# Low weight parts from a negated copy and an adding transfer, in place of a subtraction

## The chip, the core and the metric

The kernel runs on one core of a Trainium2 chip. TensorE (PE, with its weight loads as PEld), VectorE (DVE), ScalarE (ACT), GpSimd (POOL) and the queue that issues plain transfers (SP) run side by side and wait for each other by semaphores; sixteen DMA engines move data between memory and the on-chip buffers. The metric is the device time of one execution in microseconds. Three runs of the kernel before took 1635.21, 1635.33 and 1636.85 us; the median is 1635.33.

## The reference, cut to what matters

One inference step of an encoder layer with 1024 channels, for 512 prompt frames and 64 sample frames together (T = 576 columns):

```
h = LN1(alpha*x + 0.5*FFN1(x))
z = h @ w_in      # mLSTM q,k,v,o,i,f | attention q,k,v | branch gates g_m, g_a
h = LN2(alpha*h + (sig(g_m)*(mLSTM(z) @ w_ml_proj) + sig(g_a)*(Attn(z) @ w_att_proj)) @ w_out)
y = LN3(alpha*h + 0.5*FFN2(h))
```

All arrays are float32. PE multiplies in a reduced type (fp32r), so each operand is split into two: hi, the operand rounded to that type, and lo = operand - hi. A product is then three: hi*hi + hi*lo + lo*hi. This document is about how lo of the weights is made.

## The kernel before

Activations lie with channels on the 128 partitions, in eight slices of 128 channels (k = 0 to 7) and two halves of columns (256 and 320). Weights come in tiles of 128 x 1024 float32, 512 KB: for one block of 128 output channels, the eight slices side by side. `plan` lists all tiles in the order of use, as (key, source in memory): FFN1; the in-projection `("in", c)`, 72 tiles, with the narrow gate tile `"if"` among them; the attention projection `("ap", j)`, the mLSTM projection `("mp", j)` and the output projection `("o", j)`, 8 tiles each; FFN2.

`pump` (line 170) works down this list. It issues SP's load of a tile into a raw buffer (`wr`, two of them; line 178) and, later, converts it: ACT writes hi (`wh`, four buffers; `act`, line 137) and DVE writes lo = raw - hi (`wl`, four buffers; `tt`, line 140). Seven tiles, those in `PIECES`, are converted in two pieces of 512 columns; two of them, in `ON_POOL`, have lo made by POOL. The raw buffer is free for the next load when both hi and lo have been written. A pair of `wh` and `wl` is free when PE has done its last product with it (`done`). So a tile's conversion can begin when the tile four places before it has been used up.

`gemm` takes tiles and runs the products: for each slice k and each half, hi*hi, hi*lo, lo*hi into one PSUM bank, 48 matmuls for a tile. Normally it goes tile by tile. Where LN1 has finished only its first half, the first in-projection tiles go as a group, `WAVE_M`: v, k and q of the first pair of heads (`("in", 48)`, `("in", 40)`, `("in", 32)`) in turn within each slice on the first half, then the gate tile on the first half, then the same on the second half. All four tiles are held to the end of the group. They hold all four `wh` buffers, and the conversion of the next tile, `("in", 49)`, waits for the first of them.

After the group come, in this order: attention (eight head pairs, tiles v, k, q each, with scores, softmax and value products put between the in-projection's matmuls), the attention branch's gates (64 to 71), the attention projection, the mLSTM by four heads (8 tiles each), the mLSTM branch's gates (56 to 63), the mLSTM projection, the output projection with LN2, FFN2.

PE's order is written out by hand: a planner (`Order`) keeps a model of PE's time, and work that depends on other engines (transposes, scores, statistics) is put in with `later(delay, ...)`. The order on the other engines is made by a list scheduler from priorities (`hot` raises them; `pump` runs at 30, normalisation steps at 300) and a model of times. Each engine then executes its list strictly in order. ACT also copies products out of PSUM and computes all exponentials and sigmoids; POOL makes k copies (`kh`, `kl` in `dup`), two of the eight subtractions of the mean and the power -0.5 in the layer norms, and small copies and fills; in this kernel POOL issues no transfer.

Of the kernel before, what the change touches and what calls it, by code (L numbers as in the profile page):

```python
# [14 lines left out]
ALU = mybir.AluOpType  # L15
# [66 lines left out]
def tile_layer(ctx: ExitStack, tc: tile.TileContext, ins, outs):  # L82
    nc = tc.nc
    PE, ACT, DVE, POOL, SP = nc.tensor, nc.scalar, nc.vector, nc.gpsimd, nc.sync
# [12 lines left out]
    def hot(off):  # L97
        def wrap(fn):
            def run(*a, **k):
                with tc.high_priority(offset=off):  # L100
                    return fn(*a, **k)
            return run
        return wrap

    def nm(s):
        uid[0] += 1
        return f"{s}_{uid[0]}"
# [7 lines left out]
    def f(ap):  # L115
        return ap.bitcast(F32)

    def hs(t, hf):
        t0, n = HALVES[hf]
        return t[:, t0:t0 + n]  # L120
# [15 lines left out]
    def act(out, in_, func=AF.Copy, **kw):  # L136
        ACT.activation(out, in_, func, **kw)  # L137

    def tt(out, a, b, op, eng=None):
        return (eng or DVE).tensor_tensor(out, a, b, op=op)  # L140
# [18 lines left out]
    NX = 10  # L159
    PIECES = {("gu2", 0, 0), ("gu2", 0, 1), ("gu2", 1, 0), ("gu2", 1, 1), ("in", 48), ("in", 40), ("in", 32)}  # L160
    ON_POOL = {("gu2", 0, 0), ("gu2", 1, 0)}
    CP = (6, 7)
    CPF = (4, 5, 6, 7)
    GR = 450
    L_MEAN, L_STATS, L_SPREAD = 300, 1440, 4920
    plan = []
# [3 lines left out]
    @hot(30)  # L170
    def pump(limit=2):
        while True:
            c = wst["conv"]
            if wst["dma"] < min(len(plan), c + 2):
                i = wst["dma"]
                raws[i] = wpool.tile([P, 1024], F32, tag="wr", name=nm("wr"), bufs=2)
                src = plan[i][1]
                SP.dma_start(raws[i][:, :src.shape[1]], src)
                wst["dma"] += 1
                continue  # L180
            if c < wst["stop"] and c < wst["taken"] + limit and c < wst["done"] + NWB:
                raw = raws.pop(c)
                n = plan[c][1].shape[1]
                hi = wpool.tile([P, 1024], F32R, tag="wh", name=nm("wh"), bufs=NWB)
                if plan[c][0] == "if":

                    r3 = raw[:, :n].rearrange("p (k c) -> p k c", c=64)
                    h3 = hi.rearrange("p (k c) -> p k c", c=P)
                    act(h3[:, :, 0:64], r3)
                    tt(h3[:, :, 64:128], r3, f(h3[:, :, 0:64]), ALU.subtract)  # L190
                    parts[c] = (hi, None)
                else:
                    lo = wpool.tile([P, 1024], F32R, tag="wl", name=nm("wl"), bufs=NWB)
                    step = n if plan[c][0] not in PIECES else 512
                    for a in range(0, n, step):
                        act(hi[:, a:a + step], raw[:, a:a + step])
                        tt(lo[:, a:a + step], raw[:, a:a + step], f(hi[:, a:a + step]), ALU.subtract,
                           POOL if plan[c][0] in ON_POOL else DVE)
                    parts[c] = (hi, lo)
                wst["conv"] += 1  # L200
                continue
            return

    def take(key):
        c = wst["taken"]
        assert plan[c][0] == key, (plan[c][0], key)
        wst["taken"] += 1
        if wst["conv"] <= c:
            pump(1)
        assert c in parts  # L210
        later(300, pump)
        return c

    def done(c):
        del parts[c]
        wst["done"] += 1
        later(50, pump)
# [149 lines left out]
    for k0 in range(0, KT, 2):  # L367
        ww = slice(k0 * P, (k0 + 2) * P)
        for c in (0, 1, 2):
            hi, lo = parts[c]  # L370
# [14 lines left out]
    class Norm:  # L385
# [97 lines left out]
        def centre(self, hf, bc, power):  # L483
            mb = hs(self.c0, hf)
            act(mb, bc)
            with tc.issue_after(power.ins):
                for j in range(KT):
                    dh = hs(self.d[j], hf)
                    tt(dh, dh, mb, ALU.subtract, POOL if j in (CPF if self.final is not None and hf else CP) else DVE)

# [632 lines left out]
    mp = mstack.enter_context(tc.tile_pool(name="ml", bufs=1, reuse_waits="tile"))  # L1123
# [403 lines left out]
```

## Time and profile before

The profiled execution took 1635.94 us; its span, from the first to the last instruction, is 1634.2 us.

| what | value |
|---|---|
| median of three runs | 1635.33 us |
| profiled execution, its span | 1635.94 us, 1634.2 us |
| mean granted PE clock | 0.988 |
| busy: PE, DVE, ACT, POOL | 98%, 67%, 50%, 9% of the span |
| DMA engines | 27.3% of 16 engines' span, mean 90 GB/s |
| read from memory, written | 135.37 MB, 9.24 MB |
| PE idle, longest single releaser | ACT s, 9.3 us in 3 waits |

Names in the rows are tiles of the program: `wr` raw weights, `wh` and `wl` hi and lo of the weights, `mm` and `aux` PSUM banks. A row "wl<-wr,wh" writes lo from raw and hi. A value such as "[3.97 <-PE mm L123]" is the idle time of the engine just before the instruction, and what ended it. Times in rows of order are us from the span's start.

### The profile page before, as it was taken

What the parts mean: (1) busy time and instruction counts of PE and PEld (TensorE: products, weight loads), DVE (VectorE), ACT (ScalarE), POOL (GpSimd) and SP (SyncE); (2) the same over time, 40 slices, a digit from 0 to 9 for tenths busy, and PEclk for the clock granted to TensorE, in tenths of its full rate; (3) what the DMA queues carried; (4) which work ended last, traced back from release to release, by engine and by line L of the source; (5) the groups of instructions that cost most, each with busy time, mean ns of one, the idle gap of its engine ahead of it and who ended that gap; (6) DMA issues with size and microseconds to landing.
All of it is one profiled execution on the core that took longest, in us unless ns stands there. A gap on an engine that the chain in (4) does not pass through costs nothing.

```text
span 1634.2 us, 29320 instructions
## 1 busy us (share of the span) xinstructions
PE 1593.3 (98%) x11831; PEld 1567.2 (96%) x11831; DVE 1090.1 (67%) x2158; ACT 811.2 (50%) x1529; POOL 141.1 (9%) x277
## 2 busy tenths in 40 slices
PE   8999998999999999999999999999999999999997
PEld 8999998999999999999999999999999999998996
DVE  7777777535788777673656748434778777768336
ACT  6445546223566566651657466443345554545223
POOL 0000000000313323000111101002020000000001
PEclk9999999999999999999999999999989999999999
DMA  6222221224342333122222122222212222212333
GB/s 215 73 83 104 93 89 48 82 84 119 120 135 89 100 106 101 48 85 85 78 72 78 59 94 67 68 78 78 83 62 103 104 83 100 104 62 59 87 93 116
DMA packets 52320, 146.51 MB, mean 90 GB/s; under 512 B 5720, under 2 KB 16600, under 8 KB 52184
## 3 DMA queue, kind: packets, MB, share of 16 engines
q1 hardware_dynamic: 52184, 144.63, 27.3%
q8 instruction: 93, 1.52, 0.4%
q14 instruction: 43, 0.35, 0.1%
HBM read 135.37 MB, written 9.24 MB: 88 GB/s over the span
## 4 chain that ended last, share of the span: by engine, by line
PE 56%; DVE 3%; issue 1%; ACT 1%; POOL 1%; ACTq 0%; POOLq 0%; DVEq 0%
PE mm L123 51%; PE aux L123 4%; PE aux L133 1%; DVE s L140 1%; DVE h L140 0%; ACT s L137 0%; DVE wl L140 0%; DVE hc L140 0%; POOL wl L140 0%; POOL kh L147 0%; DVE s L143 0%; DVE ptl L140 0%; ACT sc L137 0%; ACT L137 0%; POOL rs L382 0%
## 5 line engine op out<-in xcount | busy, mean ns | idle before, releaser
L123 PE MATMUL mm<-s,wh 128*128 128x256 f32 (+2 forms) x3872 | 796.0, 299 | 11.4 <-ACT s L137 9.3
L123 PEld LDWEIGHTS mm<-s,wh 128*128 128x128 f32 x3872 | 624.9, 190 | 16.4 <-ACT s L137 10.1
L123 PE MATMUL mm<-s,wl 128*128 128x256 f32 (+2 forms) x1920 | 569.1, 296 | 0.0
L123 PEld LDWEIGHTS mm<-s,wl 128*128 128x128 f32 x1920 | 365.0, 190 | 0.0
L140 DVE TENSOR_TENSOR wl<-wr,wh 128x1024 fp32r<-128x1024 f32 (+2 forms) x166 | 195.9, 1183 | 186.4 <-ACT wh L137 185.8
L137 ACT ACTIVATE wh<-wr 128x1024 fp32r<-128x1024 f32 (+2 forms) x171 | 169.7, 996 | 301.5 <-PE mm L123 281.6
L123 PE MATMUL mm<-hc,wh 128*128 128x256 f32 (+1 forms) x704 | 147.7, 301 | 9.8 <-DVE hc L140 5.8
L123 PE MATMUL mm<-h,wh 128*128 128x256 f32 (+1 forms) x704 | 140.7, 294 | 0.0
L123 PEld LDWEIGHTS mm<-hc,wh 128*128 128x128 f32 x704 | 116.4, 192 | 13.2 <-DVE hc L140 8.9
L123 PE MATMUL mm<-tx,wh 128*128 128x288 f32 x624 | 128.3, 296 | 0.0
L140 DVE TENSOR_TENSOR wl<-ws,wh 128x1024 fp32r<-128x1024 f32 x39 | 47.8, 1226 | 111.1 <-ACT wh L137 111.1
L123 PEld LDWEIGHTS mm<-h,wh 128*128 128x128 f32 x704 | 112.7, 187 | 0.2
L123 PE MATMUL mm<-hc,wl 128*128 128x256 f32 (+1 forms) x352 | 105.1, 299 | 0.0
L123 PE MATMUL mm<-h,wl 128*128 128x256 f32 (+1 forms) x352 | 103.3, 294 | 0.0
L123 PEld LDWEIGHTS mm<-tx,wh 128*128 128x128 f32 x624 | 100.9, 190 | 0.0
L123 PE MATMUL mm<-tx,wl 128*128 128x288 f32 x312 | 92.8, 297 | 0.0
L137 ACT ACTIVATE wh<-ws 128x1024 fp32r<-128x1024 f32 x39 | 41.3, 1058 | 102.4 <-PE mm L123 101.7
L382 POOL TENSOR_TENSOR rs<-var,mhalf 128x2 f32<-128x2 f32 (+1 forms) x6 | 5.2, 865 | 825.0 <-DVE var L143 425.0
L123 PEld LDWEIGHTS mm<-hc,wl 128*128 128x128 f32 x352 | 67.7, 192 | 0.0
L123 PEld LDWEIGHTS mm<-h,wl 128*128 128x128 f32 x352 | 65.9, 187 | 0.0
L137 ACT ACT_TABLE_LOAD x45 | 57.7, 1283 | 5.5 <-DVE U L143 4.0
L123 PEld LDWEIGHTS mm<-tx,wl 128*128 128x128 f32 x312 | 59.1, 190 | 0.0
(282 smaller groups left out, 2864.3 us busy)
## 6 DMA issues: line engine op xcount, KB each, us to landing
wu<-in_w_gu SPq DMA_DIRECT2D x78, 512.0 KB, 4.3
wr<-in_w_in SPq DMA_DIRECT2D x72, 512.0 KB, 3.5
wr<-in_w_dn SPq DMA_DIRECT2D x40, 512.0 KB, 3.5
wr<-in_w_dn SPq DMA_DIRECT2D x20, 384.0 KB, 3.2
G<-in_rbias SPq DMA_DIRECT2D x16, 256.0 KB, 2.9
wr<-in_w_ap SPq DMA_DIRECT2D x8, 512.0 KB, 3.5
wr<-in_w_mp SPq DMA_DIRECT2D x8, 512.0 KB, 3.5
wr<-in_w_o SPq DMA_DIRECT2D x8, 512.0 KB, 3.5
```

The costliest lines, as they stand in the source:

```text
L123: PE.matmul(out, lhsT, rhs, start=start, stop=stop, **kw)
L133: PE.transpose(out, in_, idn)
L137: ACT.activation(out, in_, func, **kw)
L140: return (eng or DVE).tensor_tensor(out, a, b, op=op)
L382: return y, POOL.tensor_tensor(y, v, mhalf[:, :n], op=ALU.pow)
```

## The change

For the tiles of the in-projection (all 72), both branch projections and the output projection (24), `pump` no longer subtracts. ACT writes hi as before, then a second ACT copy writes -hi into the lo buffer, and POOL issues a transfer that reads the tile from memory a second time and adds it to what lies there: lo = -hi + w. These tiles are converted whole, the three that were in `PIECES` too. The gate tile `"if"` and the tiles of both FFNs are made as before. The raw buffer of a changed tile is read by ACT alone.

```diff
+    ADDED = ("in", "ap", "mp", "o")
...
-                    step = n if plan[c][0] not in PIECES else 512
+                    step = n if plan[c][0] not in PIECES or plan[c][0][0] in ADDED else 512
                     for a in range(0, n, step):
                         act(hi[:, a:a + step], raw[:, a:a + step])
+                        if plan[c][0][0] in ADDED:
+                            act(lo, f(hi), scale=-1.0)
+                            POOL.dma_start(lo, plan[c][1], accum_op=ALU.add)
+                            continue
                         tt(lo[:, a:a + step], raw[:, a:a + step], f(hi[:, a:a + step]), ALU.subtract,
                            POOL if plan[c][0] in ON_POOL else DVE)
```

## The prediction

> **What bounds the kernel now.** I read the page's engine totals first, then busy time by stage and the chain of waits, then the order of instructions where the changed tiles have least room.
>
> ```profile
> span 1634.2 us, 29320 instructions
> PE 1593.3 (98%) x11831; PEld 1567.2 (96%) x11831; DVE 1090.1 (67%) x2158; ACT 811.2 (50%) x1529; POOL 141.1 (9%) x277
> ...
> 418.50:445.30 26.80, 26.34 (x196) 25.82 (x195) 20.84 (x39) 12.61 (x29) 13.36 (x25) 1.00 0.31 94
> 445.30:688.00 242.70, 237.95 (x1826) 229.32 (x1825) 187.93 (x577) 157.32 (x385) 59.90 (x110) 1.00 0.32 100
> 688.00:774.00 86.00, 86.00 (x648) 85.95 (x647) 47.99 (x70) 34.35 (x48) 0.69 (x7) 1.00 0.26 83
> 774.00:1060.00 286.00, 286.00 (x2134) 278.57 (x2134) 182.76 (x392) 172.24 (x334) 32.26 (x89) 1.00 0.23 74
> 1060.00:1160.00 100.00, 98.90 (x743) 98.21 (x742) 44.11 (x68) 35.24 (x58) 13.18 (x17) 1.00 0.25 80
> 1160.00:1226.00 66.00, 63.65 (x447) 62.32 (x446) 54.16 (x119) 26.65 (x57) 10.95 (x10) 0.92 0.21 66
> ...
> PE 56%; DVE 3%; issue 1%; ACT 1%; POOL 1%; ACTq 0%; POOLq 0%; DVEq 0%
> ```
>
> A window row gives the stretch, then busy time of PE, PEld, DVE, ACT, POOL, the granted clock, the DMA share and GB/s. PE is the bound: 98% of the span, and in the chain that ended last (the last line) DVE has 3% of the span, the others less. The six stages that use the 96 changed tiles (first wave, attention, gates and attention projection, mLSTM, second gates and mLSTM projection, output and LN2) leave it idle for 0.46 + 4.75 + 0 + 0 + 1.10 + 2.35 = 8.7 us in all. That is the most that a lighter DVE could return. So the question is whether the new way of making lo makes PE wait.
>
> **The change part by part.** Per tile one DVE subtraction goes, and one ACT copy, one transfer issued by POOL and 512 KB more from memory come.
>
> ```profile
> L137 ACT ACTIVATE wh<-wr 128x1024 fp32r<-128x1024 f32 x136 | 143.9, 1060 | 215.7 <-PE mm L123 200.8 <-issue 10.7 <-DMA wr<-in_w_dn 3.3
> L140 DVE TENSOR_TENSOR wl<-wr,wh x166: 676/1224/1579, 20.8 to 1612.4; 128x1024 fp32r<-128x1024 f32 x136, 128x768 fp32r<-128x768 f32 x20, 128x512 fp32r<-128x512 f32 x10
> wr<-in_w_in SPq DMA_DIRECT2D x72, 512.0 KB, 3.5
> wr<-in_w_if SPq DMA_DIRECT2D x1, 256.0 KB, 2.7
> L178 SPq DMA_DIRECT2D wr<-in_w_in x72: 327/328/587, 406.7 to 1065.2; - x72
> ```
>
> DVE loses 96 x 1.22 = 117 us; ACT gains 96 x 1.06 = 102 us (50% to about 56%); 50 MB of loads are added. DVE is off the path, so its 117 us are worth at most the 8.7 us above.
>
> The price of the adding transfer no row shows. Below: a plain load of the same bytes lands 3.5 us after issue and its issue takes 0.33. Above: reading the weights, reading lo and writing lo one after the other, 3 x 3.5 = 10.5 us, with a POOL issue as long as its longest tile operation, 1.6 us:
>
> ```profile
> L140 POOL TENSOR_TENSOR wl<-wr,wh x4: 1296/1507/1607, 1186.4 to 1204.5; 128x512 fp32r<-128x512 f32 x4
> ```
>
> I take 5.1 us to land (3.5 plus one more pass of 512 KB at the rate of the two load rows, 2 x (3.5 - 2.7) = 1.6) and 1.0 us on POOL, inside the bounds: 6.1 us together, 3.8 to 12.1. Lo is then ready 1.06 + 6.1 = 7.2 us after hi, where DVE needed 1.22: 6 us later.
>
> **Where that is hidden.** In the pure matmul stages a tile is 48 matmuls and lasts 86.0 x 48 / 648 = 6.4 us. With four buffers, hi of a tile starts when the fourth tile before it is released, so three tiles, 19.1 us, lie between that and its use; 1.06 + 7.2 = 8.3 us fit. Attention and mLSTM put other matmuls between the tiles and have more room. The cover gone, each us beyond 19.1 would cost the 40 tight tiles (gates, second gates, three projections, 8 each) one us each.
>
> **Where it is not hidden: two places, both at the first wave.** This matmul group takes v, k, q of the first head pair and the gate tile together, in the slices of k in turn.
>
> ```profile
> 410.57 0.63 ACT L137 ACTIVATE wh<-wr 128x512 fp32r<-128x512 f32 x1 [1.53 <-DMA wr<-in_w_in]
> 417.64 1.15 ACT L137 ACTIVATE wh<-wr 128x512 fp32r<-128x512 f32 x2 [1.39 <-DMA wr<-in_w_in]
> 418.38 1.29 DVE L140 TENSOR_TENSOR wl<-wr,wh 128x512 fp32r<-128x512 f32 x2
> 418.15 0.58 POOL L799 MEMSET rows<- 128x576 f32 x1 [3.28 <-PE mm L123]
> 418.75 0.28 PE L123 MATMUL mm<-s,wl 128*128 128x256 f32 x1
> 419.11 0.28 PE L123 MATMUL mm<-s,wl 128*128 128x256 f32 x1
> 419.47 0.28 PE L123 MATMUL mm<-s,wl 128*128 128x256 f32 x1
> ```
>
> The third tile's lo is written from 418.38 and PE wants it at 419.47. After the change its raw load starts earlier, when hi of the first tile (410.57 + 1.06) frees the buffer instead of DVE's last piece, and lands near 415.4. ACT then has 3 hi and 3 lo (6.4 us) from 410.57, between LN1's activations (some 3.4 us in the same stretch):
>
> ```profile
> L137 ACT ACTIVATE s<-s,cols 128x256 fp32r<-128x256 f32 x8 | 3.7, 500 | 2.3 <-DVE s L143 2.3
> ...
> 418.70 0.49 ACT L137 ACTIVATE s<-s,cols 128x256 fp32r<-128x256 f32 x1
> ```
>
> So -hi of the third tile ends between 417.5 (weights first) and 420.4 (LN first); I take 419.0. Plus 6.1 is 425.1: PE waits 5.6 us (1.9 to 13). The transfer issue may also stand behind POOL's memsets, which end near 419.5; that is in the range. LN1's activations slip by up to 3.2 us if the weights go first; the last of them, at 418.70, is wanted for the eighth slice, 7 x 1.08 us after 418.5, so that costs nothing. Everything later is queued on PE behind this wait, LN1's second statistics too, so it is all paid.
>
> ```profile
> 441.93 2.01 ACT L137 ACTIVATE wh<-wr 128x1024 fp32r<-128x1024 f32 x2 [3.97 <-PE mm L123]
> 443.02 2.36 DVE L140 TENSOR_TENSOR wl<-wr,wh 128x1024 fp32r<-128x1024 f32 x2 [3.39 <-ACT wh L137]
> 444.81 2.42 POOL L147 TENSOR_SCALAR kh<-kf 64x576 fp32r<-64x576 f32 x2 [8.51 <-ACT kf L137]
> 445.34 0.28 PE L123 MATMUL mm<-s,wl 128*128 128x256 f32 x1
> ```
>
> The wave holds all four buffers to its end, so hi of the next tile waits for PE until 441.93, and PE wants its lo at 445.34. Now lo was ready at 444.24, 1.1 us ahead. Then: -hi ends 443.0 + 1.06 = 444.1, plus 6.1 is 450.2: PE waits 4.8 us (2.6 to 10.8). The tile after it is converted 2.1 us later on ACT and has the whole next product as cover.
>
> **The clock.** PE's gaps cost twice here:
>
> ```profile
> 42.58:45.67 3.09, 0.43 (x3) 0.21 (x2) 3.06 (x7) 1.88 (x4) 0.00 (x0) 1.00 0.00 0
> 45.67:49.08 3.41, 3.41 (x14) 3.41 (x15) 0.75 (x2) 0.85 (x2) 0.00 (x0) 0.50 0.00 0
> ```
>
> After 2.7 us without matmuls within 3.1 us, the granted clock was 0.50 for 3.41 us. I take one such stretch per stall: 1.7 us each, 3.4 together (0 to 6.8). The Trainium skill (TensorE: Matmul & The Clock Gate, The HAM clock gate) says that the rate halves after at least one idle window of about 3.4 us, with windows that run freely. By it a 4.8 us stall need not hold a whole window, and the sum below would be 10.4 to 13.8 us; the row, with less than one window idle, says 13.8.
>
> **POOL in attention, costed at nothing net.** A third of the tiles are converted while POOL makes the next k copies:
>
> ```profile
> 617.87 1.06 ACT L137 ACTIVATE wh<-wr 128x1024 fp32r<-128x1024 f32 x1
> 618.47 0.41 POOL L147 TENSOR_SCALAR kh<-kp 64x256 fp32r<-64x256 f32 x1
> 618.97 1.47 DVE L140 TENSOR_TENSOR wl<-wr,wh 128x1024 fp32r<-128x1024 f32 x1
> 619.42 1.28 POOL L147 TENSOR_SCALAR kh<-kp 64x256 fp32r<-64x256 f32 x1
> 622.94 0.75 DVE L140 TENSOR_TENSOR kl<-s,kh 64x576 fp32r<-64x576 f32 x1 [1.66 <-POOL kh L147]
> 624.08 0.66 PE L133 MATMUL aux<-ident,sc 128*128 128x128 f32 x4 [0.31 <-DVE ptl L140]
> ```
>
> Behind the new issue stand kh and kl; DVE's kl waits for them and PE's transposes for DVE's next result. The issue adds 1.0 us to POOL's burst; the subtraction beside which a kh copy took 1.28 us, where the one before it took 0.41, goes. The two cancel: 0, between -4.75 (all idle of the stage gone) and, for 7 chunks, +7 x (1.6 + 1.06) = +19 if POOL also sits waiting for -hi.
>
> **ACT in mLSTM, costed at nothing.**
>
> ```profile
> 800.00:820.00 20.00, 20.00 (x145) 19.36 (x144) 13.49 (x25) 19.66 (x32) 2.84 (x10) 1.00 0.17 54
> 820.00:840.00 20.00, 20.00 (x156) 19.60 (x155) 9.68 (x21) 8.88 (x21) 0.00 (x0) 1.00 0.31 99
> ```
>
> Three more copies (3.2 us) make ACT late in the full stretch; the next, 8.88 of 20 busy, takes them up, and a product's other pair of banks covers 6.4 us. Without that cover 4 heads x 3.2 = 13 us.
>
> **Sum.** 5.6 + 4.8 + 3.4 = 13.8 us on the profiled 1635.9 (span 1634.2, 1.7 around it) is 1649.7; the median of the runs is 0.6 lower, so 1649. Its own range: 1.9 + 2.6 = 4.5 us gives 1640; 13 + 10.8 + 6.8 = 30.6 gives 1666.
>
> **Rivals.**
>
> ```profile
> 1185.85 0.49 DVE L140 TENSOR_TENSOR s<-mm,s 128x320 f32<-128x320 f32 x1 [1.77 <-PE mm L123]
> ```
>
> - Short transfer. The Trainium skill (DMA: Bandwidth & Descriptors, Anatomy of one DMA) fits 2.0 us plus bytes over 436 KB per us for a transfer issued this way, an estimate of 3.2 us here in place of my 6.1. In terms of rows: if it costs no more than the plain load, 3.8, both waits shrink by 2.3 us to 3.3 and 2.5 and the clock may hold: 1641. For it: the 3.5 us row. Against: an add must read lo as well.
> - POOL as the bound in attention: the +19 above, on top of the two stalls: 1668. For it: PE already waits 0.31 us per chunk at the end of that chain. Against: POOL is busy only 59.9 of 242.7 us.
> - DMA throughput. At a DMA share of 0.26 a load takes 1.7 us of each 6.4. An adding transfer of up to 2.8 times that still fits; at five times, 8.3 + 1.7 - 6.4 = 3.6 us on 40 tight tiles: about 1790; at four, 1.9 x 40: 1725. Against: only one more pass is needed.
> - Faster. If both waits are at their lower bounds, +4.5, and the lighter DVE removes all 8.7 us of PE's idle time, 1631. It decides where DVE, not POOL or ACT, ends PE's waits in attention; the 0.31 us wait on ptl speaks for it, the row above against: before LN2's gaps DVE had caught up and was waiting for PE. With half the idle time recovered the two cancel: 1635.
>
> **Chances.** Two stalls near 1649: 0.50; short transfer 0.12; POOL 0.15; throughput 0.07; faster 0.09; cancelling 0.07. A measurement here tells 0.2%, 3.3 us, from no change; so faster 0.09, same 0.07, slower 0.84. The range 1635 to 1680 leaves out the faster case and the throughput case.
>
> **What would show it.** Right: PE waits of 4 to 6 us for a transfer into wl near 419 and 450, each followed by clock 0.50; no wait on wl from 460 to 1186; DVE down by 117 us, ACT up by 102. Wrong: wl waits in every tile (throughput), waits of PE's transposes over 1 us in each chunk (POOL), or no wait at the wave at all.

## The result, and the profile after

| | median of the runs | runs |
|---|---|---|
| before | 1636.09 us (1635.21 to 1636.99) | 4 |
| changed | 1656.63 us (1655.26 to 1658.14) | 4 |

The ratio is 1.0126, with a 95% interval of 1.0108 to 1.0143: the changed kernel is slower by 20.5 us. Its profiled execution took 1656.75 us, its span is 1655.0 us, 20.8 more than the 1634.2 of before.

From the page of the changed kernel: the span, the busy time of the engines, the queues of the plain loads and of POOL's transfers (packets, MB, share of sixteen engines), the bytes read and written, the shares of the chain that ended last, and the group of the new copies.

```profile
span 1655.0 us, 29495 instructions
PE 1601.1 (97%) x11831; PEld 1575.2 (95%) x11831; DVE 983.7 (59%) x2059; ACT 889.1 (54%) x1614; POOL 209.5 (13%) x373
...
q1 hardware_dynamic: 52184, 144.63, 26.7%
q0 software_dynamic: 13824, 50.34, 18.6%
...
HBM read 185.70 MB, written 9.24 MB: 118 GB/s over the span
...
PE 87%; DVE 5%; issue 3%; DMA 2%; ACT 2%; POOL 1%; SPq 0%; ACTq 0%; POOLq 0%; DVEq 0%
...
L137 ACT ACTIVATE wl<-wh 128x1024 fp32r<-128x1024 f32 x96 | 101.1, 1054 | 0.8
...
wl<-in_w_in POOLq DMA_DIRECT2D x72, 512.0 KB, 5.7
```

The change does what it says: DVE has 106 us less to do, 96 new copies of 1.05 us stand on ACT, and 50.3 MB more are read. PE is still the bound, but the DMA now has 2% of the span in the chain that ended last. (The chain of before can be followed back only to 624 us, which is 62% of the span and leaves out the wave, so the two chains cannot be set against each other share by share.) The waits of PE say where (total us, number, longest), first in the changed kernel:

```profile
PE mm L123 <- DMA wl<-in_w_in: 13.4, 4, 5.4
...
PE mm L123 <- ACT sg L137: 2.1, 1, 2.1
PE mm L123 <- ACT vf L137: 1.1, 1, 1.1
```

then in the kernel before:

```profile
PE aux L133 <- DVE ptl L140: 1.8, 6, 0.3
...
PE aux L133 <- DVE vc L140: 1.1, 6, 0.2
...
PE mm L123 <- ACT sg L137: 1.1, 1, 1.1
```

PE waits for an adding transfer four times in the whole execution, for 13.4 of the 20.8 us. Two short waits for ACT are new or longer; the small waits for DVE in attention (`ptl`, `vc`) are gone. In order of time, the third tile of the first wave (ACT's copy of -hi, POOL's transfer, PE's first products with each lo), the place of `("in", 49)`, and the second gates:

```profile
418.89 1.06 ACT L137 ACTIVATE wl<-wh 128x1024 fp32r<-128x1024 f32 x1
```
```profile
420.25 0.86 POOL L201 DMA_DIRECT2D wl<-in_w_in  x1 [2.36 <-ACT wl L137]
```
```profile
420.36 0.39 PE L123 MATMUL mm<-s,wl 128*128 128x256 f32 x1 [1.01 <-DMA wl<-in_w_in]
...
423.57 0.58 PE L123 MATMUL mm<-s,wl 128*128 128x256 f32 x1 [2.59 <-DMA wl<-in_w_in]
...
428.92 0.58 PE L123 MATMUL mm<-s,wl 128*128 128x256 f32 x1 [4.34 <-DMA wl<-in_w_in]
```
```profile
459.77 0.51 PE L123 MATMUL mm<-s,wh 128*128 128x256 f32 x2 [1.08 <-ACT vf L137]
465.71 0.58 PE L123 MATMUL mm<-s,wl 128*128 128x256 f32 x1 [5.44 <-DMA wl<-in_w_in]
```
```profile
1083.34 0.50 PE L123 MATMUL mm<-s,wh 128*128 128x256 f32 x2 [2.14 <-ACT sg L137]
```

The third transfer is issued at 420.25 and PE goes on at 428.92. The same product began at 419.47 before: PE is 9.45 us behind. At `("in", 49)` it is 20.37 behind (465.71 against 445.34). The windows of the changed kernel (PE, PEld, DVE, ACT, POOL, granted clock, DMA share, GB/s) show what lies between these two besides the waits:

```profile
422.00:439.07 17.07, 11.16 (x47) 10.47 (x48) 5.29 (x12) 0.61 (x2) 9.90 (x22) 0.50 0.54 160
...
462.90:469.73 6.83, 4.02 (x19) 4.02 (x19) 3.18 (x6) 3.57 (x6) 0.88 (x1) 0.50 1.05 281
...
1084.20:1087.61 3.41, 3.41 (x18) 3.41 (x18) 2.77 (x4) 2.30 (x5) 0.00 (x0) 0.51 0.76 132
```

The granted clock is halved for 17 us at the wave, for 6.8 us at the next place and for 3.4 us behind the 2.14 us wait at the gates. It was 1.00 throughout these stages before.

The 11,831 matmuls of the two traces, laid beside each other in order, give the account, as PE's delay against before:

| place | us | delay after it |
|---|---|---|
| difference already there at the wave's start | 0.45 | 0.45 |
| three waits for lo at the wave (1.01 + 2.59 + 4.34) | 7.94 | |
| half clock around and behind them | 5.03 | 13.42 |
| wait for ACT's `vf`, and small ones | 1.24 | 14.66 |
| wait for lo of `("in", 49)` | 5.44 | |
| half clock around and behind it | 2.15 | 22.25 |
| attention: 0.6 us gained at its start and about as much in each of its later steps | -4.91 | 17.34 |
| small waits at its end | 0.41 | 17.75 |
| the other gates, the projection and the mLSTM | 0.00 | 17.75 |
| second gates: 1.1 more wait for ACT's `sg`, then half clock (1.5) | 2.58 | 20.33 |
| the rest | 0.45 | 20.78 |

The expectations below put the delay after the wave's two stalls at 21.8 and the gain in attention at 4.4; the rows give 22.25 and, on balance, 4.5.

### The profile page after: what moved, and what is told of

It is laid out like the page before. It is cut to its first block, busy times and chain, and to the rows that moved or that the text cites. A ratio compares the mean times of both kernels' runs of the same rounds, so it can differ in the third digit from the quotient of the medians.

```text
span 1655.0 us, 29495 instructions
## 1 busy us (share of the span) xinstructions
PE 1601.1 (97%) x11831; PEld 1575.2 (95%) x11831; DVE 983.7 (59%) x2059; ACT 889.1 (54%) x1614; POOL 209.5 (13%) x373
## 3 DMA queue, kind: packets, MB, share of 16 engines
q1 hardware_dynamic: 52184, 144.63, 26.7%
q0 software_dynamic: 13824, 50.34, 18.6%
## 4 chain that ended last, share of the span: by engine, by line
PE 87%; DVE 5%; issue 3%; DMA 2%; ACT 2%; POOL 1%; SPq 0%; ACTq 0%; POOLq 0%; DVEq 0%
PE mm L123 78%; PE aux L123 7%; PE aux L133 2%; DMA wl<-in_w_in 1%; DVE h L140 1%; DVE s L140 1%; DVE wl L140 1%; DVE sc L989 1%; ACT wh L137 0%; ACT sc L137 0%; DVE hc L140 0%; DMA wr<-in_w_gu 0%; ACT s L137 0%; DVE vc L140 0%; DMA s<-in_xT 0%
## 5 line engine op out<-in xcount | busy, mean ns | idle before, releaser
L123 PE MATMUL mm<-s,wl 128*128 128x256 f32 (+2 forms) x1920 | 572.7, 298 | 13.4 <-DMA wl<-in_w_in 13.4
L140 DVE TENSOR_TENSOR wl<-wr,wh 128x1024 fp32r<-128x1024 f32 (+2 forms) x67 | 74.1, 1110 | 103.4 <-ACT wh L137 103.2
L137 ACT ACTIVATE wl<-wh 128x1024 fp32r<-128x1024 f32 x96 | 101.1, 1054 | 0.8
L201 POOL DMA_DIRECT2D wl<-in_w_in x72 | 63.3, 880 | 285.8 <-ACT wl L137 211.3
```

Source lines behind the costliest of these rows:

```text
L123: PE.matmul(out, lhsT, rhs, start=start, stop=stop, **kw)
L201: POOL.dma_start(lo, plan[c][1], accum_op=ALU.add)
```

## The experiments

The variants with another set of tiles choose the ones that are made with the adding transfer by a function in place of the test on `ADDED`; the others are subtracted as before. Where a ratio stands, it is against the kernel before, run on the same chip.

**All but four tiles added.**

```diff
+    def added(key):
+        return key[0] in ADDED and key not in (("in", 48), ("in", 40), ("in", 32), ("in", 49))
```

> Only the four tiles at the first wave (v, k, q of head pair 0 and v of pair 1) keep the old subtraction; the other 92 keep the adding transfer. My theory (waits and clock at the wave are the loss, attention gains): the wave's 21.8 us go, attention's gain of 4.4 and the later losses of 0.6 at 675 and 2.8 at 1064 to 1068 stay: 1635 us, within 2. Rival (the transfers load the DMA engines or POOL and everything pays a little): the loss goes in proportion to the tiles, 4 of 96, so about 1656.

Measured: 1635.94 us (10 runs; before 1636.55), ratio 0.9994 [0.9985, 1.0004]. With 92 of 96 tiles still added the whole loss is gone. So it belongs to these four tiles; on balance, the other 48 MB of transfers cost nothing.

**Only those four added.**

```diff
+    def added(key):
+        return key in (("in", 48), ("in", 40), ("in", 32), ("in", 49))
```

> Only the four tiles at the first wave use the adding transfer, all others the old subtraction. My theory: the whole of the wave's loss, 21.8 us, and no gain in attention: 1658 us, within 2, so slower than with all 96 tiles changed. Rival (loss in proportion to the tiles): about 1637.

Measured: 1658.10 us, ratio 1.0126 [1.0111, 1.0141]. Four tiles cost as much as 96. Its waits of PE:

```profile
PE mm L123 <- DMA wl<-in_w_in: 15.9, 4, 7.7
...
PE aux L133 <- DVE ptl L140: 2.9, 6, 0.6
```

The small waits for DVE's `ptl` in attention are there again: where the attention tiles are subtracted, the gain is missing. The wait for `("in", 49)` is longer here, 7.7 us in place of 5.4.

**All but five added.** The fifth is `("in", 61)`, whose copy of -hi stands ahead of the sigmoids at the second gates.

```diff
+    def added(key):
+        return key[0] in ADDED and key not in (("in", 48), ("in", 40), ("in", 32), ("in", 49), ("in", 61))
```

> As the run with four tiles subtracted, and the in-projection tile whose second ACT copy stands before the gate sigmoids near 1080 subtracted too. My theory: PE's wait for the sigmoid falls from 2.14 to 1.09 us and the half-rate clock after it (3.4 us long, 1.5 us lost) goes: 2.5 us less than the run with four, 1632.5, faster than before by 3.5 us. Rival (the later sigmoid is not due to this copy): same time as the run with four.

Measured: 1634.17 us (9 runs; before 1636.55), ratio 0.9981 [0.9971, 0.9991]: faster than before, and the expected time lies inside the interval. The wait at the gates is back at its old size, and the half clock behind it is gone. First the wait, then the window that holds it and the one behind it:

```profile
PE mm L123 <- ACT sg L137: 1.1, 1, 1.1
```
```profile
1057.00:1063.00 6.00, 4.93 (x34) 4.21 (x33) 4.64 (x11) 3.63 (x7) 0.98 (x1) 1.00 0.00 0
1063.00:1070.00 7.00, 7.00 (x56) 7.00 (x55) 5.45 (x8) 6.29 (x13) 0.00 (x0) 1.00 0.20 75
```

In the changed kernel's profile this copy of 1.06 us on ACT cost 1.1 us of waiting and 1.5 us of halved clock. The wait is shown to hang on the copy; the clock behind it is less certain. The version with four subtracted tiles has the same wait of 2.14 us (at 1066.32), and its clock stayed at 1.00, so its profile and this one differ by the 1.1 us alone at the gates.

**PE kept busy while it waits.** As the changed kernel, with 10, 26, 44 and 56 products of a constant tile, whose result nobody reads, ahead of the first use of each of the four lo tiles.

```diff
+                                fill = FILL.pop(tiles[t][c][0], 0)
+                                if fill:
+                                    spare = bank()
+                                for _ in range(fill):
+                                    PE.matmul(spare[:, 0:P], ones_r, ones_r, start=True, stop=True)
```

> All 96 tiles as in the change; before the first use of each of the four late tiles PE gets products of a constant into a spare bank, about as long as its wait there. Their results are not used. My theory: the waits stay, the clock stays at full rate at the wave, so 7.6 us less than the change: 1649 us, clock 1.0 from 420 to 470. Rival (the loss is waiting alone, the clock costs little): 1656 or more.

Measured: 1654.27 us, ratio 1.0101 [1.0086, 1.0116]; the changed kernel has 1.0126 [1.0108, 1.0143]. Windows of this kernel, at the wave, at `("in", 49)` and at the second gates:

```profile
418.00:440.00 22.00, 21.40 (x175) 20.80 (x174) 7.50 (x17) 4.63 (x9) 12.85 (x27) 1.00 0.69 181
...
459.00:475.00 16.00, 16.00 (x132) 15.80 (x131) 8.72 (x28) 14.01 (x26) 3.00 (x4) 1.00 1.02 263
...
1078.00:1090.00 12.00, 10.77 (x61) 10.77 (x62) 5.53 (x8) 8.56 (x17) 0.70 (x1) 0.72 0.35 80
```

and the last of these in the changed kernel:

```profile
1078.00:1090.00 12.00, 9.84 (x60) 9.12 (x59) 7.28 (x16) 9.00 (x15) 1.01 (x2) 0.86 0.39 87
```

The clock stays at 1.00 at both stalls, and the transposes of the first scores, at 458.93 before and 480.26 in the changed kernel, begin at 475.85: 4.4 us are saved, 5.3 if one counts that this execution was 0.9 us later than that of the changed kernel at the wave's start. But the half clock at the gates is longer here (0.72 against 0.86), and the total moved by 2.4 us, and the two intervals overlap. So the clock's share at the stalls is shown in the trace; the expected 7.6 us in the total are not. The stalls themselves stay: filled or not, PE cannot go on before the lo has landed.

**The four without their transfer.**

```diff
-                            POOL.dma_start(lo, plan[c][1], accum_op=ALU.add)
+                            if plan[c][0] not in (("in", 48), ("in", 40), ("in", 32), ("in", 49)):
+                                POOL.dma_start(lo, plan[c][1], accum_op=ALU.add)
```

Lo of these four tiles is then -hi alone.

> As the changed kernel, but ("in", 48), ("in", 40), ("in", 32) and ("in", 49) get lo = -hi alone: the adding transfer of these four is left out. Theory: the two stalls belong to the transfer. ACT's third copy ends about when PE first wants it, so a wait of at most 1 us is left at the wave and none at the tile after it, no halved clock, and the time is that of the kernel in which the four are subtracted, 1636, to 1638. Rival: ACT's own lateness (six copies and LN1 on one engine) is half of it, or the clock halves anyway: 1645 or more.

Measured: 1637.68 us (10 runs; before 1635.89), ratio 1.0013 [1.0004, 1.0023]. No wait for a lo is left; of the new waits only ACT's remain:

```profile
PE mm L123 <- ACT sg L137: 2.1, 1, 2.1
...
PE mm L123 <- ACT vf L137: 1.1, 1, 1.1
```

ACT's six copies at the wave are not what costs, but for the 1.1 us at `vf`: without the transfers the ratio falls from 1.0126 to 1.0013, by some 18.5 us.

**One tile of the wave alone.**

```diff
+    def added(key):
+        return key == ("in", 32)
```

> Added: ("in", 32) alone, the third tile of the first wave; the other 95 as before. In the changed kernel its transfer took from 420.25 to 428.92, 8.7 us, while the DMA engines were full (share 1.01): two more adding transfers, raw loads and loads for attention were in flight. Theory: it was contention of the adding transfers among themselves; alone, it lands about as the median does, 5.7 us after issue, and PE waits about 4 us for it, once. Rival: the plain loads that SP issues at the same time suffice: 7.5 us or more to land, and PE waits 6 us or more.

Measured: 1649.38 us (2 runs), ratio 1.0084 [1.0065, 1.0102]. The rival holds. POOL's issue, PE's product and the window between them:

```profile
420.34 1.07 POOL L204 DMA_DIRECT2D wl<-in_w_in  x1 [16.29 <-ACT wl L137]
```
```profile
429.33 0.58 PE L123 MATMUL mm<-s,wl 128*128 128x256 f32 x1 [9.48 <-DMA wl<-in_w_in]
```
```profile
420.34:429.33 8.99, 0.00 (x1) 0.00 (x1) 1.95 (x5) 0.97 (x3) 4.48 (x11) 0.58 0.82 236
```

A single adding transfer makes PE wait 9.5 us, longer than three did together (7.9), and with the clock its trace is 13.6 us behind at `("in", 49)`. The other two adding transfers of the wave are not what made the third slow. Beside it SP's plain loads for attention (`vp`, `kp`, `G`) and for the next tiles were in flight; they were slowed too. Transfers in 420 to 429 of this kernel (KB, median us to landing):

```profile
wl<-in_w_in POOLq DMA_DIRECT2D x1, 512.0 KB, 8.9
G<-in_rbias SPq DMA_DIRECT2D x2, 256.0 KB, 8.6
wr<-in_w_in SPq DMA_DIRECT2D x1, 512.0 KB, 8.3
```

and in 418 to 428 of the kernel before, where the same loads run without the adding transfer:

```profile
wr<-in_w_in SPq DMA_DIRECT2D x2, 512.0 KB, 3.5
G<-in_rbias SPq DMA_DIRECT2D x2, 256.0 KB, 4.3
```

That these loads and the adding transfer share the engines is the likeliest reading; a version in which SP's loads stay away from it was not tried. Another reading, that the first adding transfer of an execution is slow, does not hold: in the changed kernel the first, issued at 414.34, landed in 6.0 us, and so did the first of the version from the third pair on (below), issued at 453.79 with weight loads in flight beside it and the engines full (DMA share 1.02). Full engines alone thus did not make it slow there. The one at the wave had loads for attention beside it as well, and the slow ones around `("in", 49)`, 7.1 to 10.6 us in the changed kernel, had a store (`out_k`) and each other; which of these weighs most is open.

**Only the attention tiles added**, and **the same with DVE's subtraction kept**, into the raw buffer, where nobody reads it:

```diff
+    def added(key):
+        return key[0] == "in" and 33 <= key[1] <= 55 and key[1] not in (40, 48, 49)
...
                             POOL.dma_start(lo, plan[c][1], accum_op=ALU.add)
+                            tt(raw[:, a:a + step], raw[:, a:a + step], f(hi), ALU.subtract)
```

The first part of this edit is in both, the last line only in the second. The set has 20 tiles; the expectations say 21.

> Added: only the 21 attention tiles after the first wave, without ("in", 49). All other tiles are subtracted as before. Theory: the changed kernel's only gain, 4.4 us, lies in attention, where PE no longer waits 0.3 us a chunk for DVE, and these 21 tiles carry all of it: 1632.2 (before 1636.5 less 4.4), PE gains between 460 and 660 and keeps its lead. Rival: the gain is an accident of the order that follows the late first wave, or POOL's issues cost as much as DVE's relief returns: 1636 or more.

> As the version with only the 21 attention tiles added, but DVE still does its subtraction for them, into the raw buffer, where nobody reads it. Theory: the gain in attention is DVE's relief; with the subtraction back on DVE it is gone: 1636 to 1637, PE's 0.3 us waits for DVE's ptl are back. Rival: the gain comes from something else that the change moves (the order on ACT and POOL, the earlier release of the raw buffer is undone here too): 1632 to 1633.

Measured: 1633.93 us without the subtraction, ratio 0.9988 [0.9979, 0.9997]; 1637.59 with it, ratio 1.0011 [1.0003, 1.0020] (11 runs each; before 1635.89, 27 runs). One window of 190 us inside attention, in the kernel before, in the version without and in the one with the subtraction:

```profile
470.00:660.00 190.00, 186.63 (x1442) 180.61 (x1442) 147.70 (x444) 116.17 (x290) 52.74 (x99) 1.00 0.32 100
```
```profile
470.00:660.00 190.00, 188.99 (x1469) 184.00 (x1468) 134.31 (x430) 133.73 (x311) 63.83 (x117) 1.00 0.59 143
```
```profile
470.00:660.00 190.00, 186.93 (x1450) 181.20 (x1450) 146.93 (x443) 132.35 (x309) 69.23 (x118) 1.00 0.59 145
```

The second and the third differ above all in DVE, 134 against 147 us; ACT and the DMA share are alike. POOL is 5.4 us busier in the third, and its transfers land later there, in 7.6 us in the middle against 5.7, but PE waits for none of them in this window. PE's busy time is 2.4 us higher with the free DVE, and with the busy one it is that of before. The waits of PE for DVE go the same way, first without the subtraction, then with it:

```profile
PE aux L133 <- DVE ptl L140: 0.3, 1, 0.3
...
PE aux L133 <- DVE vc L140: 0.2, 1, 0.2
```
```profile
PE aux L133 <- DVE ptl L140: 1.6, 6, 0.3
...
PE aux L133 <- DVE vc L140: 1.1, 6, 0.2
```

So the gain in attention is DVE's relief, and the transfers and ACT's copies in between cost nothing there. In the total 2.0 of the expected 4.4 us came: at the start of attention PE lost 1.7 us, of it 1.2 in a wait for ACT's `kh` and 0.5 in one for a lo.

**Attention from the third pair on**, meant to keep the gain and lose that 1.7 us.

```diff
+    def added(key):
+        return key[0] == "in" and 34 <= key[1] <= 55 and key[1] not in (40, 41, 48, 49)
```

> Added: only the 18 attention tiles from the third head pair on, as far as v of the second, ("in", 50) to ("in", 55), 42 to 47 and 34 to 39. Theory: the version with 21 tiles lost 1.7 us before it gained, because ACT's two extra copies for k and q of the second pair stand ahead of kh and of LN1's last copy; subtracted, these cost nothing, the gain of about 3.4 us stays, and the time is 1632.5 (before 1636.0). Rival: ACT's loss only moves to the next copies, or the gain shrinks with it: 1634 or more.

Measured: 1633.04 us (11 runs; before 1636.16), ratio 0.9982 [0.9973, 0.9991]. The expected time lies inside the interval, but not for the expected reason. Waiting PE at the start of attention, in this version:

```profile
456.75 0.55 PE L133 MATMUL aux<-ident,s 128*128 128x128 f32 x3 [0.51 <-ACT s L137]
459.05 0.33 PE L133 MATMUL aux<-ident,sc 128*128 128x128 f32 x1 [1.09 <-DVE mx L992]
```

The loss moved to the next scores, as the rival had it: PE's trace stands 1.6 us ahead of before at the end of the mLSTM, against 1.8 with the 20 tiles. The rest of this profile's lead, 2.2 us, lies in the output stage, whose tiles are subtracted as before: the clock was 1.00 there, against 0.93 before, as it was with only the four tiles of the wave added. So the medians of many runs say more here than one profile. The versions with 91, 20 and 18 added tiles (ratios 0.9981, 0.9988, 0.9982) cannot be told apart; each is a little faster than both kernels of this document.

**Each transfer issued twice**, for the 91 tiles; and **the second one a tile later**, where `owed` holds it back (the last lines issue it when its own tile is about to be used). Lo has the weights twice in both.

```diff
                             POOL.dma_start(lo, plan[c][1], accum_op=ALU.add)
+                            POOL.dma_start(lo, plan[c][1], accum_op=ALU.add)
```
```diff
+                            if owed:
+                                POOL.dma_start(*owed.pop(), accum_op=ALU.add)
                             POOL.dma_start(lo, plan[c][1], accum_op=ALU.add)
+                            owed.append((lo, plan[c][1]))
...
         assert c in parts
+        if owed and owed[0][0] is parts[c][1]:
+            POOL.dma_start(*owed.pop(), accum_op=ALU.add)
```

> As the version with five subtracted tiles, but each of the other 91 tiles issues its adding transfer twice, so that its lo has the weights added twice. Theory: an adding transfer takes 3.2 us of all sixteen DMA engines (18.6% of the span over 96 tiles), so two of them and the plain load take 8.1 us of a tile that lasts 6.4: throughput binds, 1.7 us on each of the 40 tight tiles, 1634 + 68 = about 1702. Rival: only latency counts, and two transfers one after the other (13 us) still lie inside the 19 us that three buffers give: 1634 to 1640.

> As the version with each transfer issued twice, but the second one of a tile is issued after the first one of the next tile, so that POOL need not stand waiting for the first to land. (Lo has the weights added twice.) Theory: of the 179 us that the doubled transfers cost, most was POOL's wait, 8.0 us a tile, in front of the issues and copies behind it; what is left is throughput: two adding transfers and a load took 7.5 us of the sixteen engines per tile in the stretch 740 to 790, 1.1 us over a tile's 6.4, 44 us on 40 tight tiles: about 1680. Rival: the DMA engines alone set it and POOL's wait is only their shadow: 1780 or more. Rival: no limit at all once POOL is free: 1634 to 1645.

Measured: 1815.02 and 1810.17 us (2 runs each), ratios 1.1099 and 1.1067. In the second kernel the edit puts the held transfer just ahead of the next tile's first one, not behind it as the expectation has it. Groups of POOL's transfers in the first kernel (busy, mean ns, idle before), then POOL's largest wait for them in the second, then a stretch of tight tiles in the second:

```profile
L205 POOL DMA_DIRECT2D wl<-in_w_in x67 | 58.5, 873 | 443.7 <-DMA wl<-in_w_in 390.9
```
```profile
POOL wl L206 <- DMA wl<-in_w_in: 365.3, 55, 8.9
```
```profile
740.00:790.00 50.00, 44.62 (x331) 44.01 (x329) 26.02 (x39) 34.38 (x49) 10.66 (x12) 1.00 0.90 192
```

Both expected times were far off: 68 and 44 us, where 179 and 174 came. In both kernels POOL stands still until the first transfer has landed, some 6 us a tile and up to 8.9, and everything on POOL behind it stands too; 47 and 49 us of the loss lie in attention, whose tiles are long and whose k copies are POOL's, and 50 and 52 in the mLSTM. The DMA engines were 90% busy in the tight stretch. The second kernel did not take POOL's wait away, so the two causes were not separated; where throughput alone would begin to bind stays open.

## Why the prediction was right, and where its sum was not

The forecast was slower, 1649 us, within 1635 to 1680; it came to 1656.6. Step by step:

- **The two stalls at the first wave: right in place and mechanism**, though the first came in three pieces, one for each lo, where the sum has one. Of 96 adding transfers PE waits for four, all there, and for none from 466 to the end. Subtracting these four removes the whole loss; adding only these four brings all of it.
- **The size of the first stall**: 5.6 us (1.9 to 13) were predicted, 7.9 us of waits measured. Third -hi was put at 419.0 and ended at 419.95. Issue and landing were put at 6.1 us and took 8.7 from 420.25. The median of the 72 transfers, 5.7 us, is close to the assumed 6.1; the sum did not ask what else is on the DMA engines at that moment.
- **The size of the second stall**: 4.8 us (2.6 to 10.8) predicted, 5.4 measured, with 7.1 us from POOL's issue at 458.60 to PE's product:

```profile
458.60 1.84 POOL L201 DMA_DIRECT2D wl<-in_w_in  x2 [18.57 <-ACT wl L137]
```

- **The clock, the worst-sized term of loss**: 3.4 us (0 to 6.8) predicted, as one stretch of 3.41 us for each stall. The stretches were 17.07, 6.83 and 3.41 us long and cost about 5.0 + 2.2 + 1.5 = 8.7 us, the last of them behind a wait for ACT that the sum did not have. The step that failed is "I take one such stretch per stall": it took the one example in the trace, a pause of under 3.1 us, for stalls that put PE 9.5 and 5.4 us behind. The Trainium skill (TensorE: Matmul & The Clock Gate, The HAM clock gate) has the clock come back after one busy window of about 3.4 us and halve after an idle one. At the cold end the traces disagree: at the gates an idle time of 2.14 us, shorter than a window, was followed by 3.41 us at 0.51, where 1.06 us was not. At the warm end they leave it open: PE was busy again from 428.92 and the clock stayed at 0.50 until 439.07, 10 us, but twelve of the first products have a single column, and large products alone ran only from 434.07, 5.0 us before the stretch ended. At the other two places the clock was back 4.0 us (465.71 to 469.73) and 4.3 us (1083.34 to 1087.61) after PE went on.
- **Attention at zero: a term of gain that was left out.** The idle time of the stage, 4.75 us, was named as the bound; 4.5 us came back on balance. The step "the two cancel" failed: POOL's issues cost PE nothing there, and the waits for `ptl` and `vc` did hang on DVE's subtraction, as the two versions whose edits differ only in it show. Of the rival "faster", the part that the 0.31 us wait on `ptl` spoke for was true; the stalls outweighed it.
- **ACT at zero: right in the mLSTM** (PE's delay is 17.8 us at its start and at its end), **not at two other places**: one copy ahead of `vf` cost 1.1 us of wait, and one ahead of `sg` 1.1 us and a halved clock. Neither place was looked at.
- **The rivals.** The short transfer (3.8 us or less) falls: in the tight stretch from 690 to 770, with a DMA share of 0.67, the adding transfers of the changed kernel landed in 5.4 and 5.8 us:

```profile
wl<-in_w_ap POOLq DMA_DIRECT2D x8, 512.0 KB, 5.8
...
wl<-in_w_in POOLq DMA_DIRECT2D x3, 512.0 KB, 5.4
```
```profile
690.00:770.00 80.00, 79.15 (x600) 78.28 (x598) 39.20 (x85) 54.61 (x87) 9.59 (x11) 1.00 0.67 145
```

By the Trainium skill's fit (DMA: Bandwidth & Descriptors, Anatomy of one DMA) an estimate of 3.2 us for these bytes follows; these rows are above it. POOL as the bound and throughput fall for a single transfer: no wait for a lo or for `kh` from 466 on. DVE was predicted to lose 117 us and lost 106; ACT was to gain 102 and gained 78, though the new copies themselves are 101.1 us in the rows; 10 us of the difference are ACT's table loads, 37 in place of 45 (47.5 us in place of 57.7).

The sum was 13.8 us and the trace has 20.8: 0.5 were there before the wave; the waits for lo are 3.0 us longer, the clock costs 5.3 more, ACT's waits and the small remainders add 2.8, and attention gives 4.5 back: 13.8 + 0.5 + 3.0 + 5.3 + 2.8 - 4.5 = 20.9, the 20.8 but for rounding. That the total came as near as 7 us is in part luck: what was added up as loss was 11.5 us short, and the gain that was left out took 4.5 of it back.

## What to carry to other kernels

Replacing a short operation of an engine that has room by a longer chain through two other engines and a transfer costs nothing where buffers give it a head start, and its whole delay where they do not: look for the first tiles of a phase and for the places where all buffers are held, and leave those few as they were. Here five tiles of 96 decide between 20 us slower and 2 us faster. Price a transfer at the place where it is waited for, beside what is in flight there (5.2 to 10.6 us here), not by its median (5.7), and price PE's stall with the clock behind it.

## What the runs showed of the hardware that was not expected

- The landing time of the adding transfer of 512 KB went from 5.4 us (DMA share 0.67) to 8.9 us (0.82, with SP's loads beside it), and the weight load beside it took 8.3 us, where such loads took 3.5. The DMA share alone does not set it: the first one of the version from the third pair on landed in 6.0 us at a share of 1.02.
- With DVE's subtraction kept beside it, the adding transfers in attention landed in 7.6 us in the middle, against 5.7 without it, at the same DMA share of 0.59 from 470 to 660. The cause was not tested.
- One adding transfer uses the sixteen engines for 18.6% x 1655.0 / 96 = 3.2 us. A plain load of the same bytes uses them for 1.6 us: the plain queue of the changed kernel moved 144.63 MB in 26.7% of the span, 442 us, which is 1.60 us for each 0.524 MB.
- The granted clock stayed at half for some 10 us after PE went on at the wave, with three waits there (17.07 us at half in all) and with the single wait of 9.5 us of the version with one added tile (17.07 us too). So the three pieces are not the reason.
- The same wait of 2.14 us at the second gates stands in four profiles. Around its end the clock fell to half for 3.41 us in two (the changed kernel, and the four without their transfer), for 6.83 us in one (the filled waits) and not at all in one (all but four added); behind the wait of 1.1 us it stayed at 1.00 in all seven profiles that have it so. The stretches at half named here are 3.41 us long, or two or five times that.
